# Smaller GpSimd pieces, remainders read from PSUM, an earlier hand-over of queries and keys, and paired way-down triples in a macaron block

## The chip, the cores and the metric

The kernel runs on one core of one Trainium2 chip. A core has five engines with instruction streams of their own: PE (matmuls, with the weight loads PEld beside them), DVE (VectorE), ACT (ScalarE), POOL (GpSimd) and SP, which here only starts DMAs. PE writes to PSUM, in banks of 128 partitions by 512 floats; DVE and ACT read PSUM, POOL works on SBUF alone. The metric is the time of one launch on the device in microseconds. The kernel before takes 1003.58 us in the median of three runs, 1002.3 to 1006.16.

## The reference

One layer on 512 tokens of width 1024: a feed-forward block, a mixer, a second feed-forward block, and a last norm. All is float32.

```python
x = x + 0.5 * swiglu(rmsnorm(x, norm_ffn1), w_ffn1_gate, w_ffn1_up, w_ffn1_down)   # 1024 -> 2816 -> 1024
x = x + hybrid_mixer(rmsnorm(x, norm_mix), w_in, ..., w_out, rel_bias)
x = x + 0.5 * swiglu(rmsnorm(x, norm_ffn2), w_ffn2_gate, w_ffn2_up, w_ffn2_down)
return rmsnorm(x, norm_final)
```

The mixer projects to eight heads of block attention ("moba") and eight heads of a sparse attention ("nsa") with three branches: compressed keys, selected keys and a window, each a causal softmax with a relative bias, weighted by gates. For 512 tokens the selections take every block that causality allows, so the kernel computes ordinary causal attention, two softmaxes per nsa head (kinds `ks` and `kw`) beside the compressed branch, and one per moba head. The outputs of all 16 heads go through `w_out`.

## The kernel before

**Precision.** A float32 operand is kept as two: a rounded part "hi" and a remainder "lo" (lo = value − hi). A product is then three matmuls, hi·hi, hi·lo, lo·hi, a *triple* (`mm3`, L87 to L89); where one side is a weight the page shows `whi` and `wlo`. `halves` (L73) makes them for a chunk of weights of up to 128x1024: ACT rounds (L81), and the remainder is subtracted (L82) by DVE, or by POOL while `side[0]` is set, which is the whole attention stage.

**The feed-forward blocks.** The way up of the first six of 22 hidden tiles is done plainly (`pgu`, 512 columns per matmul). The other 16 go in pairs of tiles by a scheme of seven block products instead of eight, on half-width operands: `Ffn.pair` gives 14 steps per pair, two for each product, each step four triples, twelve matmuls of 256 columns, into the banks `pu`, `pv` and `pw`. The way down (`Ffn.down`) is a list of steps of one triple each, `pd`, 512 columns per matmul. `mixed` (L376) lays the way down of one group of four hidden tiles, 32 triples (36 for the first), as *fills* between the 28 steps of the next group. A weight per step spreads them; before, it looks for due fills after every step. `go` emits the steps in that order on PE, and loads and halves ahead of them.

**The attention stage.** Everything PE does here comes from two lists. The attention steps (`steps`, made from L1076 on) are three per head and kind; a step has three parts that run at different lags: logits (`ps_s`, L919 and L920), six steps later the transposes of the softmax (`ps_t`, L949, emptied by ACT at L952 and DVE at L953), nine steps later the products with the values (`po`, L93 and L94). The softmax itself is DVE (L927), ACT's exponential (L929), a reciprocal (L934) and POOL's normalisation (L940). The other list is `work`, the *filler*: projections of 8 triples (`pp`) and output projections (`pw`), 4 triples each, streamed with two weight chunks loaded ahead. `pre` is run ahead of the first logits, `fill` is meant to go between the steps, `last` needs the last heads. `share` (L1092) says how many triples of filler a step gets; `need` runs filler at once until something is there.

After its projection a query or key pair of moba heads is scaled by DVE, split into hi and lo (L604, L605) and moved by 16 small DMAs from SP (L609) to the places where a head needs it (`moba_split`). `ahead(h)` (L1051) asks for pair 1 when head 1 starts, pair 2 at head 3, pair 3 at head 5; pair p is first read by head 2p.

When a head's output `po` is complete, `out_halves` (L861) makes its hi and lo: ACT rounds the upper half of the bank (L874), DVE subtracts (L875), ACT copies the lower half of the bank to SBUF as `u` (L877), and DVE adds (L878).

Of the kernel before, what the change touches and what calls it, by code (L numbers as in the profile page):

```python
# [9 lines left out]
F32 = mybir.dt.float32  # L10
F32R = mybir.dt.float32r
AF = mybir.ActivationFunctionType
ALU = mybir.AluOpType
AX = mybir.AxisListType

S = 512
D = 1024
F = 2816
NK = D // 128
# [13 lines left out]
def block_kernel(ctx: ExitStack, tc: tile.TileContext, A: dict, out: bass.AP):  # L33
# [7 lines left out]
    nc = tc.nc  # L41
# [16 lines left out]
    def f32(ap):  # L58
        return ap.bitcast(F32)
# [11 lines left out]
    side = [False]  # L71

    def halves(src, cuts=None):  # L73

        n, width = src.shape[1:]
        hi, lo = [wp.tile([128, 1024], F32R, name=name, tag=name, bufs=3)[:, :n * width].rearrange(
            "p (a b) -> p a b", a=n) for name in ("whi", "wlo")]
        at = 0
        for cut in cuts or (n,):
            s = slice(at, cut)  # L80
            nc.scalar.activation(hi[:, s], src[:, s], AF.Copy)  # L81
            (nc.gpsimd if side[0] else nc.vector).tensor_tensor(lo[:, s], src[:, s], f32(hi[:, s]), ALU.subtract)  # L82
            at = cut
        return [(hi[:, i], lo[:, i]) for i in range(n)]

# [83 lines left out]
    class Ffn:  # L169
# [206 lines left out]
        def mixed(self, steps, fills):  # L376

            out, done = [], 0
            weight = [0 if i < 2 or i == len(steps) - 1 else 3 if i % 14 == 7 else 1 for i in range(len(steps))]
            for i, s in enumerate(steps):  # L380
                out.append(s)
                upto = sum(weight[:i + 1]) * len(fills) // sum(weight)
                out += fills[done:upto]
                done = upto
            return out
# [85 lines left out]
    with ExitStack() as ph:  # L471
        tmp = ph.enter_context(tc.tile_pool(name="tmp1", bufs=5))
# [62 lines left out]
        def then(d, p):  # L535
# [4 lines left out]
        steps, fills = begun(ffn, A["wd1"], 6, [  # L540
            (3, squares_of_tokens), (4, lambda: roots(0, ss[:, 0])), (5, lambda: rows_of_roots(0, "mm")),
            (12, make_rows)])
# [17 lines left out]
    with ExitStack() as ph:  # L560
        tmp = ph.enter_context(tc.tile_pool(name="tmp2", bufs=2))
# [18 lines left out]
        def proj(i, then):  # L580

            def body(w):
                p = pt("mm", "pp")
                for k in range(NK):
                    mm3(p, w[k], xg[k], k == 0, k == NK - 1)
                    yield
                then(p)
            return A["w_a"][i], body
# [50 lines left out]
        def nsa_q(pair):  # L639
            def then(p):  # L640
                t = scaled(p, 0.125)
                got["t", pair] = t
                if pair < 2:
                    nsa_split(pair)
            return then
# [215 lines left out]
        def out_halves(h):  # L861

            pair, odd = divmod(h, 2)
            if pair not in oT:
                if pair < 4:
                    oT[pair] = [kvn() for _ in range(2)]
                else:
                    oT[pair] = [kv.tile([128, S], F32R, name=f"o{pair}{i}") for i in range(2)]
            hi, lo = oT[pair]
            o = outs.pop(h)  # L870
            out_done.add(h)
            t = tmp.tile([128, S], F32, name="to", tag="t", bufs=6)
            b = half(odd)
            nc.scalar.activation(hi[b], o[:64], AF.Copy)  # L874
            nc.vector.tensor_tensor(t[b], o[:64], f32(hi[b]), ALU.subtract)  # L875
            u = tmp.tile([128, S], F32, name="u", tag="t", bufs=6)
            nc.scalar.activation(u[b], o[64:], AF.Copy)  # L877
            nc.vector.tensor_tensor(lo[b], t[b], u[b], ALU.add)  # L878

        QIS = ((0, 1), (2,), (3,))  # L880
        JS = ((0,), (1,), (2, 3))
# [143 lines left out]
        vproj, vhid, vsec = compress(1)  # L1025
        vn = token_major("vn", A["w_n"], 280, vn_tiles)
        vm = token_major("vm", A["w_v"], 512, vm_tiles)
        def marked(w):
# [2 lines left out]

        pre = [kproj, *vn, proj(10, nsa_k("ks")), vm[0], khid[0], vproj, khid[1], vm[1], khid[2],
               proj(11, nsa_k("kw")), khid[3], vm[2], ksec[0], vhid[0], vhid[1], proj(12, nsa_q(0)), ksec[1],
               vhid[2], vhid[3], vm[3], (None, marked)]
        fill = [proj(13, nsa_q(1)), vsec[0], proj(14, nsa_q(2)), vsec[1], proj(15, nsa_q(3))]
        for i in range(4):
            fill += [proj(2 * i, moba_t("q", i)), proj(2 * i + 1, moba_t("k", i))]
            if i >= 2:
                fill += [w_out(d, 4, 8) for d in range(4 * i - 8, 4 * i - 4)]
        both = []  # L1040
        last = [w_out(d, 0, 4, both if d < 2 else None) for d in range(NK)]
        work = stream(pre + fill + last)
# [8 lines left out]
        def ahead(h):  # L1051

            if h != 7:
                bias_tile(8 if h is None else 0 if h == 15 else h + 1)
            if h in (11, 13):
                need(("t", (h - 7) // 2))
                nsa_split((h - 7) // 2)
            if h == 15:
                need(("m", 0))
            elif h in (1, 3, 5):  # L1060
                need(("m", h // 2 + 1))

        def need(key):
# [28 lines left out]
        share = [0.6 if i < n_nsa else 0.55 for i in range(len(steps) + 9)]  # L1092
        for i in range(len(steps)):
            if i < 6:
                share[i] += 1.5
            if i in busy:
                share[i] += 4.0
            if i + 1 in starts or i + 1 == len(steps):
                share[min(i + 9, len(share) - 1)] += 2.0
            if starts.get(i) in (1, 3, 5):  # L1100
                share[i + 1] += 3.0
        for i in range(len(steps) - 1, len(steps) + 8):
            share[i] += 1.2
# [182 lines left out]
```

## Time and profile before

| | |
|---|---|
| median of three runs | 1003.58 us (1002.3 to 1006.16) |
| the profiled execution | 1002.16 us, its span 1000.4 us |
| granted clock of TensorE | 0.998 |
| PE busy | 974.6 us (97%), 5944 matmuls |
| PEld, DVE, ACT, POOL busy | 860.0, 719.5, 509.4, 154.9 us |
| first feed-forward block | to about 352 us |
| projections, then the attention steps | 352 us on; steps from 426 to 624 us |
| second feed-forward block and the last norm | from about 646 us |

A row of the timeline has the start in us from the span's start, the length in us, the engine, the line, the operation, and what it writes and reads; "[0.87 <-DVE tl L953]" means 0.87 us of idle time just before it, ended by DVE's instruction that wrote `tl`. A row of the groups has the count behind x, the total busy time and the mean in ns. Matmuls overlap: the length shown of a 512-column matmul is longer than the distance from its start to the next one's, so their pace is read from the starts. A stretch on PE without idle time can still be faster or slower.

### The profile page before, as it was taken

To read this page: it belongs to the slowest core of one execution; us is meant where nothing else is said; L and a number is where in the kernel's file an instruction comes from. 1 tells how busy PE (TensorE), PEld (TensorE's weight loads), DVE (VectorE), ACT (ScalarE), POOL (GpSimd) and SP (SyncE) were. 2 spreads that over 40 slices of the span, in tenths; PEclk is the share of its full clock that TensorE was granted. 3 is DMA by queue.
4 is the path that set the end of the run, shared out by engine and by line. 5 is a ranking of instruction groups with operands and counts; after the bars stand their busy time and mean duration, and the time that the engine had idled before them with its cause. 6 is when DMAs were issued, how large, how long until landed. Compare 5 with 4: busy or idle time off the path is not lost.

```text
span 1000.4 us, 15514 instructions
## 1 busy us (share of the span) xinstructions
PE 974.6 (97%) x5944; PEld 860.0 (86%) x5944; DVE 719.5 (72%) x1117; ACT 509.4 (51%) x869; POOL 154.9 (15%) x187
## 2 busy tenths in 40 slices
PE   9999999999999999999899889999999999999997
PEld 7889899999999898888778767888899999999995
DVE  4996676777765676688888766778866777767743
ACT  7653343444443354677766756645434444344444
POOL 0000000000000253055545534600000000000002
PEclk9999999999999999999999999999999999999999
DMA  9533266323211136742224441453343323342102
GB/s 322 225 114 114 77 199 183 107 96 105 94 64 43 57 107 175 236 121 72 66 59 122 111 111 39 129 218 105 91 143 106 93 95 105 109 126 90 39 1 85
DMA packets 45741, 113.86 MB, mean 114 GB/s; under 512 B 10049, under 2 KB 14866, under 8 KB 45668
## 3 DMA queue, kind: packets, MB, share of 16 engines
q1 hardware_dynamic: 45380, 112.73, 36.2%
q8 instruction: 47, 0.77, 0.3%
q14 instruction: 26, 0.21, 0.1%
q10 hardware_dynamic: 288, 0.14, 0.1%
HBM read 100.08 MB, written 5.30 MB: 105 GB/s over the span
## 4 chain that ended last, share of the span: by engine, by line
PE 89%; DVE 5%; DMA 2%; ACT 2%; issue 1%; POOL 1%; SPq 1%; DVEq 0%; ACTq 0%
PE pd L87 8%; PE pd L88 8%; PE pd L89 8%; PE pu L89 6%; PE pu L87 6%; PE pu L88 6%; PE pgu L88 4%; PE pgu L89 4%; PE pgu L87 4%; PE pw L87 4%; PE pw L88 4%; PE pw L89 4%; PE pp L87 2%; PE pp L89 2%; PE pp L88 2%; PE ps_t L949 2%
## 5 line engine op out<-in xcount | busy, mean ns | idle before, releaser
L197 ACT ACTIVATE sph<-aw 128x1024 fp32r<-128x1024 f32 x114 | 121.0, 1061 | 238.1 <-PE pu L88 118.2
L81 ACT ACTIVATE whi<-raw 128x1024 fp32r<-128x1024 f32 (+3 forms) x115 | 112.1, 976 | 106.3 <-PE pd L88 30.7
L198 DVE TENSOR_TENSOR spl<-aw,sph 128x1024 fp32r<-128x1024 f32 x114 | 139.3, 1222 | 35.7 <-ACT sph L197 35.7
L82 DVE TENSOR_TENSOR wlo<-raw,whi 128x1024 fp32r<-128x1024 f32 (+3 forms) x89 | 110.5, 1243 | 24.3 <-ACT whi L81 23.2
L88 PE MATMUL pd<-h,whi 128*128 128x512 f32 x320 | 126.3, 395 | 0.0
L87 PE MATMUL pd<-h,whi 128*128 128x512 f32 x320 | 126.1, 394 | 0.0
L89 PE MATMUL pd<-h,wlo 128*128 128x512 f32 x320 | 125.2, 391 | 0.0
L87 PE MATMUL pu<-th,sph 128*128 128x256 f32 x384 | 106.9, 278 | 0.0
L89 PE MATMUL pu<-th,spl 128*128 128x256 f32 x384 | 106.9, 278 | 0.0
L88 PE MATMUL pu<-tl,sph 128*128 128x256 f32 x384 | 106.7, 278 | 0.0
L287 DVE TENSOR_TENSOR aw<-aw 128x1024 f32<-128x1024 f32 x64 | 78.1, 1220 | 30.8 <-DMA aw<-in_wgu 30.7
L469 DVE SCALAR_TENSOR_TENSOR x<-pd,x 128x512 f32<-128x512 f32 x72 | 49.4, 689 | 46.5 <-PE pd L89 46.5
L88 PEld LDWEIGHTS pu<-tl,sph 128*128 128x128 f32 x384 | 72.6, 189 | 4.0
L87 PEld LDWEIGHTS pu<-th,sph 128*128 128x128 f32 x384 | 72.1, 188 | 4.3
L87 PE MATMUL pgu<-xo,whi 128*128 128x512 f32 x192 | 75.1, 391 | 0.2 <-ACT xo L123 0.2
L88 PE MATMUL pgu<-xo,whi 128*128 128x512 f32 x192 | 74.9, 390 | 0.3 <-DVE xo L124 0.3
L89 PE MATMUL pgu<-xo,wlo 128*128 128x512 f32 x192 | 74.8, 389 | 0.0
L89 PEld LDWEIGHTS pu<-th,spl 128*128 128x128 f32 x384 | 72.1, 188 | 0.0
L89 PEld LDWEIGHTS pd<-h,wlo 128*128 128x128 f32 x320 | 60.1, 188 | 13.4
L89 PE MATMUL pw<-xo,spl 128*128 128x256 f32 x256 | 70.9, 277 | 0.0
L87 PE MATMUL pw<-xo,sph 128*128 128x256 f32 x256 | 70.8, 276 | 0.0
L88 PE MATMUL pw<-xo,sph 128*128 128x256 f32 x256 | 70.8, 276 | 0.0
(254 smaller groups left out, 2451.0 us busy)
## 6 DMA issues: line engine op xcount, KB each, us to landing
aw<-in_wgu SPq DMA_DIRECT2D x64, 512.0 KB, 4.3
raw<-in_wgu SPq DMA_DIRECT2D x23, 512.0 KB, 5.6
raw<-in_wd SPq DMA_DIRECT2D x22, 512.0 KB, 3.5
raw<-in_wd2a SPq DMA_DIRECT2D x18, 512.0 KB, 3.6
raw<-in_w_a SPq DMA_DIRECT2D x16, 512.0 KB, 3.5
raw<-in_w SPq DMA_DIRECT2D x8, 512.0 KB, 3.8
kvn<-xo SPq DMA_DIRECT2D x32, 128.0 KB, 2.4
aq<-xo SPq DMA_DIRECT2D x32, 128.0 KB, 2.4
```

The lines of the kernel that those rows point to most:

```text
L81: nc.scalar.activation(hi[:, s], src[:, s], AF.Copy)
L82: (nc.gpsimd if side[0] else nc.vector).tensor_tensor(lo[:, s], src[:, s], f32(hi[:, s]), ALU.subtract)
L87: nc.tensor.matmul(p, w[0], v[0], start=first, stop=False, skip_group_check=again)
L88: nc.tensor.matmul(p, w[0], v[1], start=False, stop=False, skip_group_check=again)
L89: nc.tensor.matmul(p, w[1], v[0], start=False, stop=last, skip_group_check=again)
L197: nc.scalar.activation(hi, v, AF.Copy)
L198: nc.vector.tensor_tensor(lo, v, f32(hi), ALU.subtract)
L287: nc.vector.tensor_tensor(to, x, y, op)
L469: nc.vector.scalar_tensor_tensor(xs[d], p, 0.5, xs[d], ALU.mult, ALU.add)
L949: nc.tensor.transpose(p[:, wide:wide + 128], lps[qi][:, j * 128:(j + 1) * 128], ident)
```

## The change

Four edits.

1. While POOL makes weight remainders, it makes them block by block of a chunk, in pieces of up to 256 columns; all blocks of the chunks concerned are 128 wide, so eight instructions of 128x128 stand where one of 128x1024 stood (four for the 128x512 chunks of `w_out`).
2. In `out_halves` the copy `u` goes, and DVE's add reads the lower half of the bank itself.
3. In the attention stage the projection of the second nsa query pair moves from `fill` to `pre`; the first six steps get 0.5 more triples each than the base rate, in place of 1.5; pair p of the moba heads is asked for when head 2p − 2 starts, one head sooner; and all eight early output projections come after all projections, where four stood ahead of the last pair's.
4. `mixed` looks for due fills after every second step only.

```diff
             nc.scalar.activation(hi[:, s], src[:, s], AF.Copy)
-            (nc.gpsimd if side[0] else nc.vector).tensor_tensor(lo[:, s], src[:, s], f32(hi[:, s]), ALU.subtract)
+            if side[0]:
+                for i in range(at, cut):
+                    for c in range(0, width, 256):
+                        b = slice(c, min(c + 256, width))
+                        nc.gpsimd.tensor_tensor(lo[:, i, b], src[:, i, b], f32(hi[:, i, b]), ALU.subtract)
+            else:
+                nc.vector.tensor_tensor(lo[:, s], src[:, s], f32(hi[:, s]), ALU.subtract)
...
                 out.append(s)
+                if i % 2 == 0 and i < len(steps) - 1:
+                    continue
                 upto = sum(weight[:i + 1]) * len(fills) // sum(weight)
...
             nc.vector.tensor_tensor(t[b], o[:64], f32(hi[b]), ALU.subtract)
-            u = tmp.tile([128, S], F32, name="u", tag="t", bufs=6)
-            nc.scalar.activation(u[b], o[64:], AF.Copy)
-            nc.vector.tensor_tensor(lo[b], t[b], u[b], ALU.add)
+            nc.vector.tensor_tensor(lo[b], t[b], o[64:], ALU.add)
...
-               vhid[2], vhid[3], vm[3], (None, marked)]
-        fill = [proj(13, nsa_q(1)), vsec[0], proj(14, nsa_q(2)), vsec[1], proj(15, nsa_q(3))]
+               vhid[2], vhid[3], vm[3], proj(13, nsa_q(1)), (None, marked)]
+        fill = [vsec[0], proj(14, nsa_q(2)), vsec[1], proj(15, nsa_q(3))]
         for i in range(4):
             fill += [proj(2 * i, moba_t("q", i)), proj(2 * i + 1, moba_t("k", i))]
-            if i >= 2:
-                fill += [w_out(d, 4, 8) for d in range(4 * i - 8, 4 * i - 4)]
+        fill += [w_out(d, 4, 8) for d in range(NK)]
...
-            elif h in (1, 3, 5):
+            elif h in (0, 2, 4):
                 need(("m", h // 2 + 1))
...
             if i < 6:
-                share[i] += 1.5
+                share[i] += 0.5
...
-            if starts.get(i) in (1, 3, 5):
+            if starts.get(i) in (0, 2, 4):
                 share[i + 1] += 3.0
```

The order of instructions shows it at three places. First PE in the first feed-forward block, where fills stand between steps; before (`pw` is a step's bank, `pd` the way down):

```order
L88 MATMUL pw<-xo,sph 128x256
L89 MATMUL pw<-xo,spl 128x256
L87 MATMUL pd<-h,whi 128x512
L88 MATMUL pd<-h,whi 128x512
L89 MATMUL pd<-h,wlo 128x512
L87 MATMUL pw<-xo,sph 128x256
L88 MATMUL pw<-xo,sph 128x256
```

And PE in the same block after the change:

```order
L94 MATMUL pu<-tl_130,sph 128x256
L95 MATMUL pu<-th_129,spl 128x256
L93 MATMUL pd<-h,whi 128x512
L94 MATMUL pd<-h,whi 128x512
L95 MATMUL pd<-h,wlo 128x512
L93 MATMUL pd<-h,whi 128x512
L94 MATMUL pd<-h,whi 128x512
L95 MATMUL pd<-h,wlo 128x512
L93 MATMUL pu<-xo,sph 128x256
```

One triple after twelve matmuls of 256 columns became two triples after 24. Over both blocks the runs of `pd` among the steps were 152 of three, 32 of six and 16 of nine matmuls; they are 67 of six, 20 of nine, 12 of twelve and 4 of fifteen.

Then POOL at the start of the attention steps, before (`wlo` is a weight remainder, `lpn` and `lp` the softmax rows that are normalised):

```order
L82 TENSOR_TENSOR wlo<-raw,whi 128x1024 x2
L940 TENSOR_SCALAR lpn<-lpn,m,gates 128x128
L940 TENSOR_SCALAR lpn<-lpn,m,gates 128x256
L940 TENSOR_SCALAR lpn<-lpn,m,gates 128x384
L940 TENSOR_SCALAR lp<-lp,m,gates 128x512
L82 TENSOR_TENSOR wlo<-raw,whi 128x1024
```

And after the change:

```order
L86 TENSOR_TENSOR wlo<-raw,whi 128x128 x16
L946 TENSOR_SCALAR lpn<-lpn,m,gates 128x128
L946 TENSOR_SCALAR lpn<-lpn,m,gates 128x256
L946 TENSOR_SCALAR lpn<-lpn,m,gates 128x384
L946 TENSOR_SCALAR lp<-lp,m,gates 128x512
L861 MEMSET tb 128x256
```

Two remainders still stand ahead of the first normalisation, as 16 instructions; there were ten chunks of 128x1024 on POOL and there are nine.

Last SP at the end of the moba heads, before (`tb` is a head's bias, these rows hold the last two of 16; `aq` and `kvn` are the moves of the last query and key pair, for heads 6 and 7):

```order
L854 DMA tb<-scr_t 128x256
L68 DMA raw<-in_w_o 128x512
L609 DMA aq<-xo 64x512 x4
L68 DMA raw<-in_w_o 128x512
L609 DMA kvn<-xo 64x512 x8
L854 DMA tb<-scr_t 128x256
L68 DMA raw<-in_w_o 128x512 x7
```

And after the change:

```order
L862 DMA tb<-scr_t 128x256
L617 DMA kvn<-xo 64x512 x8
L862 DMA tb<-scr_t 128x256
L68 DMA raw<-in_w_o 128x512 x2
L862 DMA tb<-scr_t 128x256
L68 DMA raw<-in_w_o 128x512 x9
```

The eight moves of the last keys stood ahead of one head's bias and stand ahead of two, one head sooner.

## Prediction

> **What bounds the kernel now.** I read the busy time of each engine in three stretches first: one wholly inside the first feed-forward block, and the two halves of the attention stage.
>
> ```profile
> 100.00:325.00 225.00, 225.00 (x1588) 208.19 (x1587) 159.33 (x181) 93.62 (x121) 0.00 (x0) 1.00 0.35 108
> 425.00:550.00 125.00, 117.57 (x698) 99.68 (x699) 104.30 (x298) 87.52 (x227) 65.87 (x87) 1.00 0.33 89
> 550.00:655.00 105.00, 95.86 (x495) 79.48 (x493) 75.51 (x147) 67.26 (x139) 51.89 (x57) 1.00 0.38 108
> ```
>
> The columns are PE, PEld, DVE, ACT, POOL, then the granted clock. In the feed-forward block PE is never idle (225.00 of 225): there the time is the number of matmuls times their spacing, and nothing done on other engines can help. In attention PE stands still for 7.4 us and 9.1 us, with DVE busy 104.3 of 125. So the second view is who PE waits for, the same stage (total us, times, longest).
>
> ```profile
> PE ps_t L949 <- DVE tl L953: 7.0, 10, 1.1
> PE ps_s L920 <- DMA kvn<-xo: 2.5, 1, 2.5
> PE pw L88 <- DVE o L878: 1.7, 1, 1.7
> PE ps_t L949 <- DVE m L934: 1.7, 1, 1.7
> PE ps_s L919 <- DVE vm L691: 1.3, 1, 1.3
> PE pw L87 <- ACT o L874: 0.7, 1, 0.7
> ```
>
> The largest is the transpose `ps_t` waiting until DVE has emptied the bank of an earlier transpose (L953). To see what made DVE late I read the timeline of POOL, DVE and PE around single waits.
>
> ```profile
> 572.33 2.39 POOL L82 TENSOR_TENSOR wlo<-raw,whi 128x1024 fp32r<-128x1024 f32 x1 [0.50 <-ACT whi L81]
> 572.38 2.88 DVE L878 TENSOR_TENSOR kvn<-to,u 64x512 fp32r<-64x512 f32 x1
> 576.63 0.30 PE L949 MATMUL ps_t<-ident,lpn 128*128 128x128 f32 x1 [1.14 <-DVE tl L953]
> ...
> 608.47 0.68 DVE L878 TENSOR_TENSOR kvn<-to,u 64x512 fp32r<-64x512 f32 x1
> ...
> 498.52 0.30 PE L949 MATMUL ps_t<-ident,lpn 128*128 128x128 f32 x1 [1.74 <-DVE m L934]
> ...
> 478.87 0.30 PE L949 MATMUL ps_t<-ident,lpn 128*128 128x128 f32 x1 [0.71 <-DVE tl L953]
> ...
> 466.95 0.30 PE L949 MATMUL ps_t<-ident,lpn 128*128 128x128 f32 x1 [0.76 <-DVE tl L953]
> ...
> L878 DVE TENSOR_TENSOR o<-to,u 64x512 fp32r<-64x512 f32 x8 | 9.3, 1165 | 0.5 <-ACT u L877 0.4
> L875 DVE TENSOR_TENSOR to<-po,kvn 64x512 f32<-64x512 f32 x8 | 5.5, 683 | 3.3 <-ACT kvn L874 3.2
> ```
>
> The add of L878, both inputs in SBUF, starts just after POOL's 2.39 us remainder and ends after it: 2.88 us, where the same instruction later takes 0.68 with POOL silent. L875, the same shape with one input in PSUM, takes 683 ns on average in the same stretch. So I read that DVE is held until POOL's instruction ends, and that an operand in PSUM avoids it. The four PE waits above, 4.35 us, each follow such a held DVE instruction within some 3 us.
>
> **The change part by part.** The sum is made against the profiled execution's own 1002.16 us (span 1000.4), which lies 1.4 below the median of 1003.58 of the three runs (1002.3 to 1006.16).
>
> *Pieces and PSUM remainders.* 16 adds L878 lose their copy `u` and read PSUM, as L875 does; I price each at L875's 683 ns, so nothing is left to be held. The bank `po` is now given back after that add and not after ACT's copy; there are two such banks and a head fills one in many steps, so this costs nothing, or 0.68 where a bank is short. Other DVE instructions that POOL holds (the halving of queries and keys, the maximum of the compressed branch) are held for one piece. A piece's price is not in the trace:
>
> ```profile
> 591.83 1.29 POOL L82 TENSOR_TENSOR wlo<-raw,whi 128x512 fp32r<-128x512 f32 x1 [4.14 <-ACT whi L81]
> ...
> L718 POOL TENSOR_TENSOR xo<-t,pos 64x248 f32<-64x248 f32 x16 | 15.9, 994 | 23.5 <-DVE t L593 22.6
> ...
> 498.55 0.77 POOL L940 TENSOR_SCALAR lp<-lp,m,gates 128x512 f32<-128x512 f32 x1 [2.23 <-DVE m L934]
> ...
> 501.86 0.49 PE L949 MATMUL ps_t<-ident,lpn 128*128 128x128 f32 x3
> ```
>
> From 512 columns (1.29) to 1024 (2.39) a column costs 2.15 ns, which leaves 0.19 fixed: 0.46 us for 128, the value I take, since it is the same operation. The dearest near row is L718's 0.99 for 248 columns; the low end is no fixed cost, 0.28. By the Trainium skill (GPSIMD Engine Reference, Elementwise — side-by-side cycle accounting) a two-input element costs about 2.6 cycles of 1.2 GHz, 2.2 ns; by that alone the pieces would be free, while the two rows above show a fixed 0.19 beside it. Eight pieces make 3.7 us against 2.39, so a chunk ends 1.3 later, and the normalisations queued behind it on POOL (L940) too. In the place shown the last one ends at 499.32 and its transposes start at 501.86: 2.5 us of slack covers 1.3, if PE doesn't come earlier by as much. Gain: 4.35 less a tenth, 4 us.
>
> *The start.* The projection of the second query pair, 24 matmuls, now stands before the first logits. There PE waited 1.3 us for the eviction of `vm` (row above), which was held behind a DVE instruction of 2.43 us:
>
> ```profile
> 422.80 2.43 DVE L759 TENSOR_TENSOR w2l<-w,w2h 128x128 fp32r<-128x128 f32 x1 [1.20 <-ACT w2h L758]
> ```
>
> Eight triples cover that: 1.3 gained. The first six steps keep 1.1 triples each instead of 2.1, so the first transposes come earlier and may wait; this goes into the loss below.
>
> *Queries and keys one head sooner, output projection behind them.* Before, the last key projection had to be run in one piece (16 triples) and its moves were issued just ahead of the head that reads them:
>
> ```profile
> 592.68 5.05 SPq L609 DMA_DIRECT2D kvn<-xo  x8
> ...
> 603.66 0.41 PE L949 MATMUL ps_t<-ident,lpn 128*128 128x128 f32 x2 [0.75 <-DVE tl L953]
> ...
> 605.91 0.30 PE L949 MATMUL ps_t<-ident,lpn 128*128 128x128 f32 x1 [0.97 <-DVE tl L953]
> ```
>
> Eight moves take SP 5.05 us to issue, so the wait of 2.5 us on `kvn` is the issue queue. Six steps instead of three now lie between the request and the head that reads; the wait goes: 2.5. Moving the moves also passes them ahead of bias rows and weight loads on SP; weights are loaded two jobs ahead, so I cost that at nothing; without that lead it would be the 5.05 us of issue, once. After the burst the heads ran without any filler and showed the two waits above, 1.7 us, which filler now covers. The eight early output projections, which waited 1.7 and 0.7 for halves just being made (first list), come after all projections: 2.4.
>
> Shown idle gained: 4 + 1.3 + 2.5 + 1.7 + 2.4 = 11.9. The view draws a 512-column matmul 0.39 us long where the next starts 0.23 after it, so each wait is really 0.16 longer; ten of them, 1.6. Against it stand new waits behind longer POOL work and the thinner start. Bounds: nothing, and 7.5 (five chunks of 1.3 with their slack gone, one more us at the start); I take 1.5, near the low end, because the slack shown exceeds 1.3. Attention: −12.0.
>
> *Way down's triples by twos.* The same matmuls, in another order, where PE is the bound. These rows are starts of the first matmul of a run: `pd` of the way down (512 columns), `pu`, `pv`, `pw` (256 columns), early and late in the program.
>
> ```profile
> 86.42 0.40 PE L87 MATMUL pd<-h,whi 128*128 128x512 f32 x1
> 87.12 0.28 PE L87 MATMUL pv<-xo,sph 128*128 128x256 f32 x1
> 88.48 0.40 PE L87 MATMUL pd<-h,whi 128*128 128x512 f32 x1
> ...
> 94.66 0.40 PE L87 MATMUL pd<-h,whi 128*128 128x512 f32 x1
> ...
> 96.04 0.28 PE L87 MATMUL pu<-th,sph 128*128 128x256 f32 x1
> ...
> 97.46 0.40 PE L87 MATMUL pd<-h,whi 128*128 128x512 f32 x1
> ...
> 206.90 0.28 PE L87 MATMUL pu<-th,sph 128*128 128x256 f32 x1
> ...
> 212.55 0.40 PE L87 MATMUL pd<-h,whi 128*128 128x512 f32 x1
> ...
> 948.18 0.40 PE L87 MATMUL pd<-h,whi 128*128 128x512 f32 x1
> ...
> 949.56 0.28 PE L87 MATMUL pu<-th,sph 128*128 128x256 f32 x1
> ...
> 950.98 0.40 PE L87 MATMUL pd<-h,whi 128*128 128x512 f32 x1
> 951.68 0.28 PE L87 MATMUL pu<-th,sph 128*128 128x256 f32 x1
> 953.04 0.40 PE L87 MATMUL pd<-h,whi 128*128 128x512 f32 x1
> ```
>
> After three `pd` (0.70 us) twelve 256-column matmuls take 1.36 us (87.12 to 88.48, 951.68 to 953.04). After six `pd` (1.38) the same twelve take 1.42 (96.04 to 97.46, 949.56 to 950.98), and a run of 48 after six keeps that rate to its end: 5.65, 1.41 per twelve. I followed all runs of both blocks: after a single triple 150 of 151 twelves are fast, after two or three triples 41 of 41 are slow, as are all six 48s. After the change no single triple is left there, so I expect every 256-column run to be slow: 151 × 0.054 = +8.2 us. On the other hand a triple behind another costs 0.68 and not 0.70; in the order the 200 runs of three, six and nine become 103, so 97 × 0.02 = −1.9. Together +6.3, on the path that sets the end. Its ends are −1.9 (the rate doesn't follow the run before) and +8.2. The Trainium skill (TensorE: Matmul & The Clock Gate, Back-to-back issue gap) gives the isolated gap as N/2.4 + 2.5 ns, a matter of the column count alone, by which a regrouping costs 0; the rows show two gaps for the same 256 columns, 113 and 118 ns, so the rows decide.
>
> Sum: 1002.2 − 12.0 + 6.3 = 996.5.
>
> **Rivals.**
>
> *The rate stays fast.* What decides may not be the length of the `pd` run but something that goes with it in this order, and 24 matmuls after six have never run. Against it: 41 of 41. Then way down gives −1.9 in place of +6.3: 988.3. Chance 0.13.
>
> *Attention gives half back.* POOL's chunk is longer, the slack behind it was 2.5 us with PE late; a PE that no longer waits comes 1 to 2 us earlier and finds the normalisation not done, and DVE, at 104 of 125, keeps its other waits. For it: most `ps_t` waits are near 1 us, the size of 1.3. Then −6.0 in place of −12.0: 1002.5. Chance 0.20.
>
> *POOL becomes the bound* (the other side). If a piece costs what L718's rows do, 0.99, a chunk takes 8.0 us, 5.6 more; less 2.5 of slack each of the nine chunks makes PE wait 3.1, 28 us in all: 1024. It makes the kernel slower by over 0.5% from 0.78 us per piece (9 × (8 × 0.78 − 4.9) = 12). Against it: L718 ran beside two-input DVE work, and the undisturbed rows of L82 give 0.46. Chance 0.05.
>
> **How the numbers follow.** The main case has 0.62; its own range is 992 to 1001.5. A measurement can tell 0.5%, 5 us, from no change, so faster means below 998.6. Of the main case 0.49 lies there and 0.13 within; the fast rate is faster with all its 0.13; half given back is 0.04 faster and 0.16 the same. Faster 0.66, same 0.29, slower 0.05. The range of 988 to 1003.5 holds the main case, half of the first rival and most of the second, 0.8 in all.
>
> **What would show it.** Right: twelve-per-1.41 in every 256-column run of both blocks, a feed-forward stretch some 3 us longer in each; adds on L884 all near 0.68; POOL rows of 128 columns near 0.46; no wait on `kvn` from DMA; PE idle in attention from 16.5 to about 6. Wrong: 256-column runs at 1.36; `ps_t` waits that follow a late normalisation with POOL's pieces right before it; waits at the first transposes above 2 us.

## The result, and the profile after

| | before | after |
|---|---|---|
| median, same chip | 1004.95 us (1002.3 to 1008.33, 6 runs) | 995.35 us (993.59 to 997.19, 6 runs) |
| ratio, 95% interval | | 0.9903 (0.9877 to 0.9928) |
| profiled execution, span | 1002.16, 1000.4 us | 994.5, 992.7 us |

The change makes the kernel about 1% faster. Read from the starts of the first matmul of each stage, the two profiled executions differ like this (us):

| stage, from first matmul to first matmul | before | after | difference |
|---|---|---|---|
| span's start to the first pair step (`pu`) | 82.18 | 82.54 | +0.36 |
| pair steps and way down, first block (`pu` to `pp`) | 269.52 | 272.75 | +3.23 |
| projections and attention (`pp` to the second block's `pgu`) | 294.38 | 279.79 | −14.59 |
| the second block's plain steps (`pgu` to `pu`) | 75.32 | 75.81 | +0.49 |
| pair steps and way down, second block (`pu` to `px`) | 233.71 | 236.80 | +3.09 |
| the rest | | | −0.25 |

The same three views as before, now of the kernel after. First the busy time by stretch (PE, PEld, DVE, ACT, POOL, then the granted clock). The attention steps begin later, because a projection has moved ahead of them, so the stretches are cut at 433 and 635.

```profile
100.00:325.00 225.00, 225.00 (x1564) 209.01 (x1564) 158.06 (x179) 93.75 (x121) 0.00 (x0) 1.00 0.35 107
433.00:550.00 117.00, 113.63 (x679) 96.92 (x677) 94.40 (x290) 82.36 (x215) 75.93 (x148) 1.00 0.33 88
550.00:635.00 85.00, 84.67 (x452) 70.85 (x451) 61.82 (x146) 54.80 (x127) 50.25 (x98) 1.00 0.34 95
```

In the feed-forward stretch PE is busy throughout, as before, but 225 us now hold 1564 matmuls on record where they held 1588. In attention PE's idle time has fallen from 16.5 us to 3.7, and nearly all that is left lies in the first half. (Cut alike in both kernels, from the first logits to the second block's first matmul, it is 15.6 and 3.7 us; for the projections ahead of the logits it is 1.5 and 0.6.)

Next, who PE waits for, over the whole kernel:

```profile
PE ps_t L955 <- DVE tl L959: 2.9, 5, 1.3
PE wake L487 <- DVE ones L113: 1.5, 1, 1.5
PE pgu L93 <- ACT xo L129: 0.9, 1, 0.9
PE pc L746 <- DVE wlo L88: 0.6, 1, 0.6
PE pgu L94 <- DVE xo L130: 0.6, 2, 0.3
PE ps_t L955 <- POOL lp L946: 0.4, 1, 0.4
```

The wait for the DMA `kvn` is gone, as are those for `o` and `vm`; the wait for `tl` has fallen from 7.0 to 2.9. The only new wait of the kind that the prediction feared, a transpose behind POOL's normalisation `lp`, is 0.4 us once.

Then the adds and POOL's pieces, as groups of instructions (shape, count, busy us, mean ns):

```profile
L884 DVE TENSOR_TENSOR kvn<-to,po 64x512 fp32r<-64x512 f32 x8 | 5.5, 691 | 0.3
L884 DVE TENSOR_TENSOR o<-to,po 64x512 fp32r<-64x512 f32 x8 | 5.5, 691 | 0.3
...
L86 POOL TENSOR_TENSOR wlo<-raw,whi 128x128 fp32r<-128x128 f32 x136 | 64.6, 508 | 50.4 <-ACT whi L81 50.4
```

All 16 adds now take 0.69 us; the eight into `o` had a mean of 1.17. A piece takes 0.51 on average, and eight in a row in the attention steps take 3.55, so 0.44 each:

```profile
475.91 3.55 POOL L86 TENSOR_TENSOR wlo<-raw,whi 128x128 fp32r<-128x128 f32 x8 [0.63 <-ACT whi L81]
```

Last the rows by which the prediction priced the way down by twos: the start of the first matmul of each run, late in the second block.

```profile
931.62 0.40 PE L93 MATMUL pd<-h,whi 128*128 128x512 f32 x1
933.01 0.28 PE L93 MATMUL pv<-xo,sph 128*128 128x256 f32 x1
935.83 0.40 PE L93 MATMUL pd<-h,whi 128*128 128x512 f32 x1
937.22 0.28 PE L93 MATMUL pw<-xo,sph 128*128 128x256 f32 x1
940.05 0.40 PE L93 MATMUL pd<-h,whi 128*128 128x512 f32 x1
```

Six `pd` take 1.39 us, then 24 matmuls of 256 columns take 2.82 or 2.83, which is 1.41 per twelve. Followed over both blocks, every run of 256-column matmuls among the pair steps keeps this pace or a slower one (117.5 ns or more from start to start). All 2688 of them together take 316.75 us; before they took 308.64. That is +8.1, on PE, without any idle time to show for it. The 1056 matmuls of the way down take 220.4 us in place of 222.0, since they have fewer starts of runs.

### The profile page after: what moved, and what is told of

Read it like the earlier page. It is cut to its first block, busy times and chain, and to the rows that moved or that the text cites. A ratio compares the mean times of both kernels' runs of the same rounds, so it can differ in the third digit from the quotient of the medians.

```text
span 992.7 us, 15609 instructions
## 1 busy us (share of the span) xinstructions
PE 978.9 (99%) x5944; PEld 867.7 (87%) x5944; DVE 705.4 (71%) x1118; ACT 499.3 (50%) x853; POOL 169.3 (17%) x297
## 4 chain that ended last, share of the span: by engine, by line
PE 89%; DVE 2%; DMA 2%; POOL 2%; ACT 2%; SPq 1%; issue 1%; ACTq 0%; DVEq 0%; POOLq 0%
PE pd L93 8%; PE pd L94 8%; PE pd L95 8%; PE pu L95 6%; PE pu L93 6%; PE pu L94 6%; PE pgu L94 4%; PE pgu L95 4%; PE pgu L93 4%; PE pw L95 4%; PE pw L93 4%; PE pw L94 4%; PE ps_t L955 2%; PE pp L93 2%; PE pv L95 2%; PE pp L94 2%
## 5 line engine op out<-in xcount | busy, mean ns | idle before, releaser
L86 POOL TENSOR_TENSOR wlo<-raw,whi 128x128 fp32r<-128x128 f32 x136 | 64.6, 508 | 50.4 <-ACT whi L81 50.4
L93 PE MATMUL pw<-xo,sph 128*128 128x256 f32 x256 | 72.0, 281 | 0.0
L94 PE MATMUL pw<-xo,sph 128*128 128x256 f32 x256 | 71.9, 281 | 0.0
```

The lines of the kernel that those rows point to most:

```text
L86: nc.gpsimd.tensor_tensor(lo[:, i, b], src[:, i, b], f32(hi[:, i, b]), ALU.subtract)
L93: nc.tensor.matmul(p, w[0], v[0], start=first, stop=False, skip_group_check=again)
L94: nc.tensor.matmul(p, w[0], v[1], start=False, stop=False, skip_group_check=again)
```

## The experiments

The theory to test was the prediction's: attention gains some 12 us from waits that go, and the pairing of triples gives 6 of them back, because the length of the 512-column run ahead sets the pace of the 256-column run. The rival on the loss was that something else in the new order sets the pace; the rival on the gain, that only one part of the change does the work. "The kernel with single triples" (`singles`) is the kernel after without edit 4, and most later runs start from it. The runs come from three groups, each on one chip with its own runs of the kernel before: 1003.67 us (11 runs) for the first four, 1004.17 (21) for the next four, 1005.55 (11) for the last four.

**`singles`: the change without its pairing.**

```diff
                 out.append(s)
-                if i % 2 == 0 and i < len(steps) - 1:
-                    continue
                 upto = sum(weight[:i + 1]) * len(fills) // sum(weight)
```

> The changed kernel with the way down's triples spread as before (one where one is due, after every step). Theory, that the length of the 512-column run just ahead sets the pace of the 256-column run behind it: the twelves after a single triple take 1.36 us again, the 256-column matmuls of both blocks 308.6 us in place of 316.7, 6.3 us off the whole after 1.9 is paid back, so 989.0 beside 995.35. Rival, that the regrouping is neutral or a gain and all the rest came from attention: the same or 1.9 slower, 995 to 997.

Measured: 988.91 us (988.05 to 989.48, 5 runs), ratio 0.985 (0.9837 to 0.9863); against the 995.35 of the kernel after that is 6.4 less, by the two ratios 5.3. The loss in the sum is real, and taking edit 4 out beats both kernels. Its 256-column runs took 308.64 us, as before the change.

**`twos_only`: the kernel before with that edit alone.**

```diff
                 out.append(s)
+                if i % 2 == 0 and i < len(steps) - 1:
+                    continue
                 upto = sum(weight[:i + 1]) * len(fills) // sum(weight)
```

> The kernel before with nothing but the pairing of the way down's triples. Theory: every 256-column run slow, 6.3 us slower than before, a ratio near 1.006. Rival, pairing saves run starts: 1.9 us faster, ratio 0.998.

Measured: 1010.6 us (1009.91 to 1011.9), ratio 1.0068 (1.0056 to 1.008): +6.9 over its 1003.67. The price of the pairing is the same with and without the other edits, as far as the runs can tell. The trace has the same 316.75 us for the 2688 matmuls, and the same two stretches longer, by 3.2 and 3.1.

**`port_only`: the kernel before with the pieces and the PSUM remainders (edits 1 and 2).**

```diff
+            if side[0]:
+                for i in range(at, cut):
...
-            u = tmp.tile([128, S], F32, name="u", tag="t", bufs=6)
-            nc.scalar.activation(u[b], o[64:], AF.Copy)
-            nc.vector.tensor_tensor(lo[b], t[b], u[b], ALU.add)
+            nc.vector.tensor_tensor(lo[b], t[b], o[64:], ALU.add)
```

> The kernel before with the pieces on POOL and the remainders read from PSUM, and with neither the new plan of attention nor the pairing. Theory: the 4.35 us of waits behind held DVE instructions go, with 0.16 each hidden in the row, 4 to 6 us faster, ratio 0.995. Rival, that PE meets another late DVE instruction anyway and the longer POOL chunk costs normalisations: under 1 us.

**`plan_only`: the kernel before with the new attention plan (edit 3).**

```diff
...
-        fill = [proj(13, nsa_q(1)), vsec[0], proj(14, nsa_q(2)), vsec[1], proj(15, nsa_q(3))]
+        fill = [vsec[0], proj(14, nsa_q(2)), vsec[1], proj(15, nsa_q(3))]
...
-            if i >= 2:
-                fill += [w_out(d, 4, 8) for d in range(4 * i - 8, 4 * i - 4)]
+        fill += [w_out(d, 4, 8) for d in range(NK)]
...
-            elif h in (1, 3, 5):
+            elif h in (0, 2, 4):
...
```

> The kernel before with the attention plan alone: second query pair ahead of the logits, pairs one head sooner, early output projections after all projections, new shares. POOL's remainders whole, the copy kept, triples single. Theory: the waits on the moved keys, on the output halves, on vm and of the heads without filler go, 8 to 9 us faster, ratio 0.991. Rival, that the thinner start and the held DVE take most of it back: 3 us.

Measured: `port_only` 998.98 us (997.29 to 1000.83, 6 runs), ratio 0.995 (0.9937 to 0.9962), so −4.7; `plan_only` 992.07 (990.86 to 994.5, 4 runs), ratio 0.9884 (0.9871 to 0.9898), so −11.6, more than was expected. Added they would be −16.3; `singles`, which has both, is −14.8. So neither does the work alone; the overlap of some 1.5 us is no larger than the spread of the runs.

Their profiled executions can't be laid side by side stage by stage. Two stretches of `port_only` show why (the clock is the third figure from the end), with the wait that ends in the second:

```profile
556.00:559.40 3.40, 3.40 (x10) 2.72 (x11) 1.25 (x2) 1.12 (x2) 2.30 (x6) 0.50 0.40 136
593.60:600.40 6.80, 6.29 (x24) 5.73 (x25) 3.70 (x11) 3.08 (x9) 1.38 (x3) 0.50 0.38 96
594.11 0.45 PE L924 MATMUL ps_s<-kvn,aq 128*128 128x128 f32 x1 [2.63 <-DMA kvn<-xo]
```

In that execution the granted clock fell to 0.50 for 3.4 us and for 6.8 us, the second time while PE waited for `kvn`; in the rest of attention it was 1.00. Half of these 10.2 us, some 5 us, is an upper estimate of what it cost; this execution is the longest of the six. The mean clock alone doesn't order them (997.34 us at 0.995, 999.51 at 0.998), so the medians above are what counts.

**`one_per_24`: the kernel after with one triple after every second step instead of two or more; the rest of a group's triples stand in bulk at its end.**

```diff
-                if i % 2 == 0 and i < len(steps) - 1:
+                if i < len(steps) - 1:
+                    if i % 2:
+                        out += fills[done:done + 1]
+                        done += 1
                     continue
```

> The changed kernel with exactly one triple after every second step and what is left of a group's triples in one piece at its end, so 103 runs of 24 follow a run of three 512-column matmuls. Theory: the 24 stay fast to their end, 2.72 us, the 256-column matmuls 305.6 us in place of 316.7, about 11 us off, 984. First rival, a run is fast only for some dozen matmuls: 2.77, 990. Second rival, the length of the 256-column run itself decides: 2.83, no change, 995.

**`half_steps`: the kernel after with pair steps cut in halves of six matmuls and at most one triple per place.** Where no triple falls between the products S2 and S3, the copy `u2` is taken only after S3's first half has been added to the bank, so this kernel computes another sum there; the amount of work is the same.

```diff
-                for m in range(2):
-                    steps.append(Step(1.36, ...
+                for m, ks in ((0, (0, 1)), (0, (2, 3)), (1, (0, 1)), (1, (2, 3))):
+                    steps.append(Step(0.68, ...
...
-            weight = [0 if i < 2 or i == len(steps) - 1 else 3 if i % 14 == 7 else 1 for i in range(len(steps))]
+            weight = [0 if i < 4 or i >= len(steps) - 2 else 1 for i in range(len(steps))]
```

> The changed kernel with the steps of the pairs cut in halves of six matmuls and never more than one triple in a place, so nearly every 256-column run (6, 12 or 48 long) follows a run of three. Theory: all fast but two runs of 36, 305.0 us in place of 316.7; every triple is a run of its own at 0.70, 3.2 back; 8.5 off, 987, 2 below the kernel with single triples as before. Rival: runs of six and more starts cost something that no trace has shown, no better than 989.

Measured: `one_per_24` 1004.07 us (1000.91 to 1007.58, 10 runs), ratio 0.9999 (0.9984 to 1.0013); `half_steps` 999.86 (997.64 to 1003.78, 10 runs), ratio 0.9965 (0.9951 to 0.9979). Both missed what the theory expected of them, by 20 and by 13 us, in the same way. In `one_per_24` the list of PE's waits shows one that no kernel so far had (total, times, longest):

```profile
PE pu L93 <- ACT wc L309: 12.5, 16, 0.8
```

And its timeline shows the first of the 16 places:

```profile
95.77 0.40 PE L93 MATMUL pd<-h,whi 128*128 128x512 f32 x1
...
97.45 0.39 PE L93 MATMUL pu<-th,sph 128*128 128x256 f32 x1 [0.83 <-ACT wc L309]
97.67 0.28 PE L94 MATMUL pu<-tl,sph 128*128 128x256 f32 x1
...
98.26 0.28 PE L93 MATMUL pu<-th,sph 128*128 128x256 f32 x1
98.37 0.28 PE L94 MATMUL pu<-tl,sph 128*128 128x256 f32 x1
...
100.30 0.40 PE L93 MATMUL pd<-h,whi 128*128 128x512 f32 x1
...
101.00 0.28 PE L93 MATMUL pw<-xo,sph 128*128 128x256 f32 x1
...
103.72 0.40 PE L93 MATMUL pd<-h,whi 128*128 128x512 f32 x1
```

The triple at 95.77 should take 0.70; the next product begins 1.68 later. It goes into the same bank `u` that ACT must first copy out. In the kernels before and after the weight 3 at `i % 14 == 7` puts several triples at just this place, and my edits had removed it. Fifteen of the 16 triples cost 0.98 more than they should and one 0.83: 15.5 us, most of the miss of 20. In `half_steps` the same wait stands nine times. The theory on the pace is not touched: 24 matmuls after three `pd` take 2.72 (101.00 to 103.72), at 113 ns, in all places but those behind such a stall. What fell is my belief that triples can be placed anywhere.

**`spread`: `half_steps` from the kernel with single triples, with S2 put ahead of S1, so that two products into `u` never follow each other.**

```diff
...
+                    ("u", "S2", "T2", False, lambda: copied("u", "u2")),
                     ("w", "S1", "T1", True, lambda: copied("w", "w1")),
-                    ("u", "S2", "T2", False, lambda: copied("u", "u2")),
                     ("u", "S3", "T3", False, c22),
...
```

> The kernel with single triples, with its pair steps cut in halves of six matmuls, never more than one triple at a place (264 runs of three among the steps), and the product of S2 put ahead of that of S1, so that two products into the same bank u never follow each other. In the two earlier orders with single triples PE waited, mostly 1.0 us at a time, for ACT's copy wc of that bank, since the three triples that stood there had gone. Theory (the run of 512-column matmuls before sets the rate, three being fast however long the 256-column run is, and the wait was the copy's): all 2688 matmuls of 256 columns at 113.3 ns, 304.6 us in place of 308.6, so -4.0; 65 more run starts of 0.015, +1.0; no wait on wc; 988.9 - 3.0 = 985.9 us. Rival (a place between two products that is filled with little work makes PE wait for some other eviction): waits stay, 992 to 998. Rival (more changes of width cost PE more than the rate gives): 989 or above without a wait.

Measured: 985.84 us (984.91 to 986.1, 4 runs), ratio 0.9796 (0.977 to 0.9823), the fastest kernel of this study. PE's waits hold none on `wc`:

```profile
PE ps_t L959 <- DVE tl L963: 2.9, 5, 1.3
PE wake L491 <- DVE ones L113: 1.5, 1, 1.5
PE pR L162 <- DVE rc L156: 0.6, 1, 0.6
PE ps_t L959 <- POOL lp L950: 0.4, 1, 0.4
PE pgu L94 <- DVE xo L130: 0.3, 1, 0.3
```

The starts of the runs show the pace with six and with twelve matmuls after a triple:

```profile
133.86 0.40 PE L93 MATMUL pd<-h,whi 128*128 128x512 f32 x1
134.56 0.28 PE L93 MATMUL pu<-th,sph 128*128 128x256 f32 x1
135.24 0.40 PE L93 MATMUL pd<-h,whi 128*128 128x512 f32 x1
135.94 0.28 PE L93 MATMUL pu<-th,sph 128*128 128x256 f32 x1
137.30 0.40 PE L93 MATMUL pd<-h,whi 128*128 128x512 f32 x1
```

Six take 0.68 and twelve 1.36. The 2688 matmuls take 305.2 us, 3.5 less than in `singles`, and the stretches from each block's first pair step to the projections and to the end are together 2.9 shorter; −3.0 was worked out, as −4.0 for the pace and +1.0 for more run starts. `half_steps`, with the same halves but S2 behind S1, takes 9.6 us more in its `pd` runs and 3.4 more in its 256-column runs: most of that is the price of the wait on the copy.

**`singles_whole` and `singles_copy`: edits 1 and 2 undone one at a time.**

```diff
-            if side[0]:
-                for i in range(at, cut):
...
+            (nc.gpsimd if side[0] else nc.vector).tensor_tensor(lo[:, s], src[:, s], f32(hi[:, s]), ALU.subtract)
```

> As the kernel with single triples, but POOL makes each chunk's remainders in one instruction again; the adds read PSUM. Theory: those adds can't be held any more, but the splits of queries and the maximum of the compressed branch are, up to 2.3 us: 1 to 3 us slower than single triples with pieces, 990 to 992. Rival, with the adds on PSUM the pieces are of no more use and only lengthen POOL: 0 to 1 us faster.

```diff
-            nc.vector.tensor_tensor(lo[b], t[b], o[64:], ALU.add)
+            u = tmp.tile([128, S], F32, name="u", tag="t", bufs=6)
+            nc.scalar.activation(u[b], o[64:], AF.Copy)
+            nc.vector.tensor_tensor(lo[b], t[b], u[b], ALU.add)
```

> As the kernel with single triples, but with the copy u and the add from SBUF again; POOL in pieces. Theory: an add is held for one piece at most, 0.46 us, and ACT has 16 copies more: 0 to 1.5 us slower, 989 to 990.5. Rival, that the copy itself was a link of the chain that ends at the output projection: 3 us or more.

Measured: whole remainders 992.55 us (991.18 to 992.88), ratio 0.9884 (0.9869 to 0.99), 3.6 more than `singles` by the medians and 3.4 by the ratios, where 1 to 3 were expected; the copy `u` back 989.2 (987.99 to 990.11), ratio 0.9853 (0.9837 to 0.9869), no difference. With whole remainders PE's largest wait grows again:

```profile
PE ps_t L947 <- DVE tl L951: 5.1, 5, 2.4
```

What is held there is no add but the split of a projected pair (L605, in `singles` L611), a subtraction with both inputs in SBUF. First the rows of `singles_whole`, the longest wait included, then the same split in `singles`:

```profile
486.72 2.40 POOL L82 TENSOR_TENSOR wlo<-raw,whi 128x1024 fp32r<-128x1024 f32 x1
487.69 1.97 DVE L605 TENSOR_TENSOR xo<-t,xo 128x512 fp32r<-128x512 f32 x1
492.00 0.45 PE L947 MATMUL ps_t<-ident,lpn 128*128 128x128 f32 x1 [2.40 <-DVE tl L951]
...
488.01 0.87 DVE L611 TENSOR_TENSOR xo<-t,xo 128x512 fp32r<-128x512 f32 x1
```

So the pieces do the work of the two edits in this plan. These rows fit the Trainium skill (SBUF — State Buffer, SBUF: two separate sides), by which GpSimd and a DVE operation with two SBUF inputs exclude each other for a whole instruction: the wait shrinks with the length of the instruction that holds. Part of the 3.6 may be the clock: in the profiled execution it was 0.50 from 491.6 us on, for 3.4 us, behind this wait.

The PSUM operand saves nothing measurable, with the pieces or without. With them, the adds of the copy kernel (`singles_copy`) are hardly longer:

```profile
L884 DVE TENSOR_TENSOR o<-to,u 64x512 fp32r<-64x512 f32 x8 | 6.3, 790 | 0.2
```

That is 790 ns with the copy against 691 with the operand in PSUM, 0.1 us eight times, off the path. Without them, `plan_only` is the same kernel as `singles_whole` with the copy in place, and takes 992.07 against 992.55 (the ratio is 0.9884 for both). Its longest add shows why (min, median, max in ns):

```profile
L878 DVE TENSOR_TENSOR o<-to,u x8: 673/776/955, 465.3 to 566.6; 64x512 fp32r<-64x512 f32 x8
```

In the new plan no add meets a whole remainder; in the kernel before three of 16 did, and took 1.54, 2.83 and 2.88 us. What the PSUM operand alone would gain with the old plan, no run shows.

**`late_heads`, `early_w_out` and `late_proj`: the three moves of edit 3 undone one at a time.**

```diff
-            elif h in (0, 2, 4):
+            elif h in (1, 3, 5):
...
-            if starts.get(i) in (0, 2, 4):
+            if starts.get(i) in (1, 3, 5):
```

> The kernel with single triples, but the moba pairs' queries and keys asked for when they were before the change (at heads 1, 3 and 5), with their extra share. By the prediction's terms the wait on kvn (2.5), two bare-head waits (1.7) and 0.16 for each of these three come back: +4.7, 993.6 us. Rival (the DMA wait came from the early output projections' weight loads on the same queue, which stay away): 988.9 to 990.5, no wait on kvn.

```diff
-        fill += [w_out(d, 4, 8) for d in range(NK)]
+            if i >= 2:
+                fill += [w_out(d, 4, 8) for d in range(4 * i - 8, 4 * i - 4)]
```

> The kernel with single triples, but the eight early output projections stand ahead of the last pairs' projections as before the change. By the prediction's terms the waits for the halves just made (1.7 and 0.7, and 0.16 for each) come back: +2.7, 991.6 us. Rival (those waits came from POOL's whole remainders, which are in pieces now): 988.5 to 989.5. Third: the last pair is late by four projections and its moves wait as before: above 993.

```diff
-               vhid[2], vhid[3], vm[3], proj(13, nsa_q(1)), (None, marked)]
-        fill = [vsec[0], proj(14, nsa_q(2)), vsec[1], proj(15, nsa_q(3))]
+               vhid[2], vhid[3], vm[3], (None, marked)]
+        fill = [proj(13, nsa_q(1)), vsec[0], proj(14, nsa_q(2)), vsec[1], proj(15, nsa_q(3))]
...
-                share[i] += 0.5
+                share[i] += 1.5
```

> The kernel with single triples, but the projection of the second query pair among the fillers and 1.5 extra triples in the first six steps, as before the change. By the prediction's terms the wait for vm comes back, 1.3 and 0.16: 990.4 us. Rival (the thin start costs as much as the wait, in first transposes that wait for normalisation): 988.0 to 989.0.

Measured, beside `singles` at 988.91 and its ratio of 0.985 from the first group of runs:

| undone | median | ratio, 95% | span (`singles` 987.1) |
|---|---|---|---|
| one head sooner | 990.11 us | 0.9835 (0.981 to 0.986) | 986.4 |
| output projections last | 996.64 us | 0.9911 (0.9888 to 0.9933) | 994.7 |
| moved projection | 987.21 us | 0.9814 (0.9786 to 0.9841) | 984.4 |

With the new order in place, asking one head sooner is worth nothing that can be measured, and without it no wait on `kvn` comes back. What carries edit 3 is the order of the output projections: with the four of them back ahead of the last pair's projections the kernel is some 7 us slower (7.7 by the medians, 6.1 by the ratios). Its PE waits more on DVE, and for `m` and `o`, which the list of `singles` doesn't have; `kvn` isn't on its list either:

```profile
PE ps_t L953 <- DVE tl L957: 3.9, 6, 1.3
PE ps_t L953 <- DVE m L938: 3.1, 5, 0.8
...
PE pw L94 <- DVE o L882: 1.2, 1, 1.2
PE pw L93 <- ACT o L880: 0.9, 1, 0.9
```

In its timeline the last pair's 48 projection matmuls run in one piece (`pp`, 572.30 to 583.19, with no attention step among them), because `need` runs them at once when the pair is asked for. After them one triple of filler follows and then none until 601.60: there are output projections left, but the burst has used up the shares of the steps behind it. The busy times of that stretch, 585 to 600 us, first of `early_w_out`:

```profile
585.00:600.00 15.00, 12.22 (x83) 10.25 (x81) 14.69 (x45) 13.10 (x36) 7.37 (x15) 1.00 0.43 107
```

then of `singles`:

```profile
585.00:600.00 15.00, 15.00 (x86) 12.88 (x85) 11.79 (x30) 9.92 (x25) 9.22 (x20) 1.00 0.12 36
```

Without filler the steps are bound by DVE: it is busy 14.69 of 15 us and PE waits 2.8. With filler between the steps DVE's work has time to be done, and PE never stops.

The moved projection, with the smaller shares of the first six steps, costs rather than gains. Rows of `singles`: the first projection, the first logits, and the second block's first matmul.

```profile
352.30 0.39 PE L93 MATMUL pp<-xo,whi 128*128 128x512 f32 x1
...
429.68 0.22 PE L923 MATMUL ps_s<-kvn,aq 128*128 128x128 f32 x1
...
632.63 0.39 PE L93 MATMUL pgu<-xo,whi 128*128 128x512 f32 x1
```

The same rows of `late_proj`:

```profile
352.20 0.39 PE L93 MATMUL pp<-xo,whi 128*128 128x512 f32 x1
...
425.26 0.22 PE L923 MATMUL ps_s<-kvn,aq 128*128 128x128 f32 x1
...
629.92 0.39 PE L93 MATMUL pgu<-xo,whi 128*128 128x512 f32 x1
```

Ahead of the logits the move costs 4.3 us (77.4 against 73.1), with 21 more projection matmuls there; three of the 24 stand ahead of the logits in both. Within the steps the same matmuls cost only 1.7 (204.7 against 203.0): PE's idle time from the first logits on is 2.8 us in `late_proj` and 4.3 in `singles`, whose first transposes wait 0.9 for POOL. By these two executions the price of the move is 2.6. The kernels `after`, `half_steps` and `spread`, which have the attention code of `singles`, take 279.1 to 279.9 us from `pp` to `pgu` where it takes 280.3 and `late_proj` 277.7, so the price lies between 1.4 and 2.6; the medians give 1.7. A kernel that joins `spread` with this one would be some 2 us below 986 by these numbers; that is an estimate, it wasn't run.

## Why the prediction was right

The forecast was 996.5 and the median is 995.35; both halves of the sum hold. In the profiled executions, against which the sum was made, −5.7 was forecast and −7.7 measured.

*Way down by twos, +6.3.* Measured: +3.23 and +3.09 in the two stretches, 6.3, and +6.9 and 5.3 to 6.4 by the runs that add and remove the edit. Of its two terms, the pace was +8.2 and measures +8.1, and the fewer run starts were −1.9 and measure −1.7. The run before a 256-column run does set its pace, whatever that run's own length: 12, 24 and 48 after six or more `pd` are slow, six, 12, 24 and 48 after three are fast.

*Attention, −12.0.* Measured −14.6 for projections and attention together. PE's idle time in the steps went from 16.5 to 3.7, where about 6 was forecast, since the 1.5 set aside for new waits was hardly needed: POOL's normalisation makes PE wait 0.4 us. Idle time that the rows show makes 12.8 of the 14.6, from 17.1 to 4.3 us between the first projection and the second block; the other 1.8 fits the 1.6 that the prediction added for the drawn length of a matmul. The total came near, but its shares did not hold, so part of that is luck:

- Pieces and PSUM remainders, 4: without the pieces it is 3.6 more, and in the new plan it is the pieces alone. The prediction read the hold right and the remedy half wrong: "an operand in PSUM avoids it" is true of the adds, yet no add needed it there. Its row of 0.68 us was not "with POOL silent" (a normalisation, L940, starts at 608.20), but adds with POOL idle take 0.67 to 0.69 too. The price of a piece, 0.46, measures 0.44 in a row and 0.51 on average.
- Queries and keys one head sooner, 2.5 for `kvn` and 1.7 for bare heads: this was credited to the wrong move. With the new order, undoing the sooner request brings back neither (`late_heads`). Either move takes the wait on `kvn` away: it stands in `port_only`, which has neither (2.6), and not in `early_w_out`, which has the request without the order (and the moved projection, too). The burst and the bare heads stay in `early_w_out`, so they belong to the order: four output projections stood ahead of two projections that were due.
- Output projections behind the rest, 2.4: mis-sized for the same reason. Undone alone, it costs 7 (6 to 8).
- The start, 1.3 gained: wrong in sign; it costs 1.4 to 2.6. The wait for `vm` that it was to cover came from a DVE instruction held for 2.43 us; with pieces the same instruction takes 0.51, and neither `port_only` nor `late_proj` has that wait, though neither has the move:

```profile
423.26 0.51 DVE L765 TENSOR_TENSOR w2l<-w,w2h 128x128 fp32r<-128x128 f32 x1 [1.15 <-ACT w2h L764]
```

So undoing the parts one at a time gives 3.6 for the pieces, nothing for the adds, nothing for the sooner request, 7 for the order and some −2 for the start: 8 to 9 of the 14.8 that `singles` gains. The wait on `kvn` (2.6 us) is one part of the rest, since it comes back only where two moves are undone together. Another may be the clock: the six runs of `port_only` have mean granted clocks of 0.993 to 0.998, the five of `singles` 0.998 to 0.999. How the remaining 3 to 4 us divide stays open.

*The rivals.* A pace that stays fast is excluded by the rows above. Attention giving half back would have shown waits behind late normalisations; there is one, of 0.4, and attention gained more than the forecast. POOL as the bound would have needed 0.78 per piece; it is 0.51.

## What to carry to other kernels

Where PE is busy throughout, the order of its matmuls still has a price: look at the distance between starts, not at idle time, and try the shorter regular mixture before the longer runs. Where a stage has filler work, keep what is due first and what is free last, so that a due job never runs in a burst and leaves the steps behind it bare. A weight that looks arbitrary in a table may be the cover of one particular wait; move it only with the order that makes it needless.

## What the runs showed of the hardware

The distance between 256-column matmuls is 113.3 ns after a run of three 512-column matmuls and 117.8 after six or more, and it holds to the end of the run: 24 after three take 2.72 us, 24 after six 2.82, and 48 after three in `spread` keep 113.3. Behind a stall of 0.83 us the first few go at the slow pace and then turn fast, within one run (97.67 to 98.26 five in 0.59, 98.26 to 98.37 one in 0.11). The Trainium skill (TensorE: Matmul & The Clock Gate, Back-to-back issue gap) gives the isolated gap as a matter of the column count alone; here the same 256 columns have two gaps, 4.5 ns apart. What decides it inside PE no run here shows.

In four profiled executions (`port_only`, `plan_only`, `twos_only` and `singles_whole`) the granted clock fell to 0.50 within attention, seven times in all, for 3.4 us each and once for 6.8. Each time it began within 4 us of the start of a pause of PE of 1.3 to 2.6 us: in `singles_whole` PE stands still from 489.6 to 492.0, and the clock is 0.50 from 491.6 to 495.0. In the other ten it was 1.00 throughout that stage. Not every pause brings it on, for the profiled execution of the kernel before has the wait of 2.5 us for `kvn` at a clock of 1.00; what decides it, no run here shows. By an estimate from these rows, 3.4 us at half the clock cost up to 1.7 us, which a wait on PE can cost on top of its own length; two single executions can differ by up to 5 us in that stage from this alone, as `port_only` with its 10.2 us.
